# First norms that reuse the kept 1 / rms of the layer above, and a new order of NSA's fillers

## The chip, the cores and the metric

The kernel runs on one core of one Trainium2 chip. The metric is the device time of one execution in microseconds; the median of the timed runs is compared. Engines are named as in the profile: PE is TensorE's matmul, PEld its weight load, DVE VectorE, ACT ScalarE, POOL GpSimd, SP SyncE.

## The reference

A trunk of four layers over 256 tokens of width 1024, batch 1, in float32. Layers 0 and 3 mix tokens by differential attention ("diff"), layer 1 by native sparse attention ("NSA"), layer 2 by forgetting attention ("fox"). Each layer does the same around its mixer:

```python
for i in range(DEPTH):
    g = norm_g[i]
    h = rmsnorm(x, g[0])                    # the "first norm"
    y = mixer_i(h)                          # diff, NSA, fox, diff
    x = x + rmsnorm(y, g[1])
    y = sqrelu_mlp(rmsnorm(x, g[2]), mlp_w1[i], mlp_w2[i])
    x = x + rmsnorm(y, g[3])
    x = x + sigmoid(x @ ple_gate_w[i]) * (p[i] @ ple_w[i])   # the embedding

def rmsnorm(x, g):
    return x * lax.rsqrt(mean(x * x, axis=-1) + 1e-6) * g
```

Diff and fox project h to queries, keys and values (three blocks of 1024 columns; fox has 16 more for the forget gate, to which a bias is added before a log-sigmoid). NSA projects to 16 query heads, six blocks of 256 columns (keys and values for the compressed, selected and window branches) and 48 gates. Its compressed branch runs blocks of 32 tokens through a small two-layer network and takes a softmax over 15 of them; its three branches are added under the gates. With 256 tokens every selection block is chosen, so that the selected branch is plain causal attention.

Since every projection of h is linear and 1 / rms is one number per token, a projection can also be made of x times any per-token factor times g, if each token's result is corrected afterwards.

## The kernel before

Tokens lie in two tiles of 128 (t = 0, 1). Activations that go into a product are turned by TensorE transposes (L256) and split into a high and a low float32r part, `hT` (ACT L263 writes the high part, DVE L264 the low one). Weights arrive in `raw` tiles by SP's queue and are split in the same way by ACT (L150, `wh`) and DVE (L151, `wl`). A product is three passes (`three`, L173 to L175): high by high, low by high, high by low. PSUM is used in three rings of banks: `acc` (4), `pj` (2), `wk` (2).

The order of instructions on each engine follows from the order in which the program creates them and from the framework's scheduler, which moves an instruction ahead when it reckons it ready. `after(...)` puts each instruction of a block behind a given one on its own engine. Within a step the program's own lists set the order: `SEQ` for diff and fox (a letter for a projection, two digits for a softmax item, `p` for a step of the embedding's product `ple_proj`), `ORDN` for the items of NSA and `FILL` for what is done behind each NSA item:

- `s10`: first part of the compressed softmax of pair 1, token tile 0 (scores L959, bias L962, minimum, exp L968 on ACT, sum L970, gate, product L976 into a buffer `pc` that POOL clears, L974; there are two such buffers). `t10`: its transposes (L982), which free the buffer.
- `q1`: half of a query projection; `p`: a step of the embedding's product, for the later ones six matmuls and one ACT copy (L1145); `c`, `g`, `d`: the compressed branch's network; `O`: a weight unit of the output projection.

An NSA item computes scores (L1005), adds the bias and takes the minimum on DVE (L497), takes exp on ACT (L501); three steps later (`DP[1]` is 3) DVE scales by gate over sum (L1022), TensorE transposes (L1025), ACT copies out (L1027) and TensorE multiplies by the values (L1034).

The first norm of layer i + 1 is made in `prenorm` at the end of layer i, when the embedding's gate has been added to x (L1160): ACT squares and sums x (L220), POOL adds epsilon (L234) and takes the power of minus a half (L235), DVE multiplies x by g (L291), and the two halves are multiplied by 1 / rms on DVE (L295) or on ACT (L297), as the table `NORM` says for the layer. Then come the transposes. The result 1 / rms stays in `self.norm[t]`; the layer's second norm (`midnorm`, L309) already scales x by that kept number and corrects later.

Layer 0's first norm is special: its `hT` holds x times g without 1 / rms, and `self.cor[t]` holds 1 / rms. `cor_row` (L514 to L525) spreads both columns into a row `rb` along the tokens: the identity times `cor[t]` on DVE (L522), a matmul by ones (L523), a copy (L525). The copies out of PSUM then correct: V with `scale=cor[t]` on ACT (L534), queries and keys in `evac` by a DVE multiply by `rb` (L510). When `cor` is empty, as in layers 2 and 3, `evac` is an ACT copy (L512). NSA does not call `evac`: its queries (L947) and its selected and window keys (L990) are ACT copies.

Of the kernel before, what the change touches and what calls it, by code (L numbers as in the profile page):

```python
# [14 lines left out]
AF = mybir.ActivationFunctionType  # L15
ALU = mybir.AluOpType
AX = mybir.AxisListType

P = 128
D = 1024  # L20
S = 256
# [3 lines left out]
NH = 16  # L25
# [8 lines left out]
PACC = {0: 1, 1: 1, 2: 1, 3: 1}  # L34
PCB = 2
CW = 2
FILL = {-2: 'q0.c.p.q0.c', 1: 'p.g', 2: 'd0.q1.s01.d1', 3: 's00', 4: 't00.q1', 5: 's10.p.s11', 6: 'p', 7: 't01', 11: 't11.t10.O', 16: 'p'}
NORM = {0: 1, 1: 2, 2: 3, 3: 3}
MEP = 1
BANKS = dict(acc=('acc', 4), pj=('pj', 2), wk=('wk', 2))  # L40
MIXS = {0: {'v': 3, 'o': 2, 'd': 0, 'g': 0}, 1: {'v': 6, 'o': 2, 'd': 8, 'g': 1}, 2: {'v': 3, 'o': 6, 'd': 1, 'g': 0}, 3: {'v': 6, 'o': 2, 'd': 0, 'g': 0}}
# [45 lines left out]
class Trunk:  # L87
# [197 lines left out]
    def prenorm(self, t, g, hT, lag=()):  # L285

        nc = self.nc
        x = self.x[t]
        xn = self.s4([P, D])
        r = self.rms_kept(t, (self.rms(x), 0.0))  # L290
        nc.vector.tensor_tensor(xn, x, g, op=ALU.mult)  # L291
        for n in range(2):
            v = self.half(xn, n)
            if NORM[self.i] == 1 or NORM[self.i] == 3 and n:
                nc.vector.tensor_scalar(v, v, r, None, op0=ALU.mult)  # L295
            else:
                nc.scalar.activation(v, v, AF.Copy, scale=r)  # L297
        self.transpose_split(xn, hT[0], hT[1], t, lag=lag)

    def midnorm(self, t, g, hT, lag=()):  # L300

# [241 lines left out]
    def diff(self, i, ia, hT):  # L543
        nc, a = self.nc, self.a
        w_in = a["da_w_in"][ia]
        def between():
            if self.late is not None:
                self.late()
                self.late = None
            if self.row is None:  # L550
                self.bias_rows()

        vs = self.v_proj(w_in, 2 * D, hT, between)
        lam_init = 0.8 - 0.6 * math.exp(-0.3 * i)
# [112 lines left out]
    def fox(self, i, hT):  # L667
# [14 lines left out]
        lf = self.small([P, 2, NH])  # L682

        def forget():
            pf = self.pj()
            for k in range(KD):
                self.three(pf[:NH, :S], (wfh[:, k, :], wfl[:, k, :]), self.both(hT, k), k == 0, k == KD - 1)
            z = self.mid([NH, S])
            nc.vector.tensor_scalar(z, pf[:NH, :S], bf, None, op0=ALU.add)
            za = self.mid([NH, S])  # L690
            nc.vector.scalar_tensor_tensor(za, z, -1.0, z, op0=ALU.mult, op1=ALU.max)
            nc.scalar.activation(za, za, AF.Exp, scale=-1.0)
            nc.scalar.activation(za, za, AF.Ln, bias=1.0)
            nc.vector.scalar_tensor_tensor(za, z, 0.0, za, op0=ALU.min, op1=ALU.subtract)
            pl = self.wk()
            for t in range(2):
                nc.tensor.transpose(pl[:, t * NH : (t + 1) * NH], za[:, t * P : (t + 1) * P], self.ident[:NH, :NH])
            nc.vector.tensor_copy(lf.rearrange("p a b -> p (a b)"), pl[:, : 2 * NH])
# [145 lines left out]
    def nsa(self, i, hT):  # L844
# [21 lines left out]
        for t in range(2):  # L866
            y = self.acc()
            for k in range(KD):
                self.three(y[0][:, :256], self.tok(hT, k, t), w_vs[k], k == 0, k == KD - 1)
            for k in range(KD):  # L870
                self.three(y[1][:, :304], self.tok(hT, k, t), w_vw[k], k == 0, k == KD - 1)
            for z in range(2):
                nc.scalar.activation(vs[t][:, z], y[z][:, :256], AF.Copy)
            nc.vector.tensor_copy(gp[:, t, :], y[1][:, 256:304])
            o = self.pj()
            for k in range(KD):
                self.three(o, self.tok(hT, k, t), w_kv[k], k == 0, k == KD - 1)
            kv = self.m2([P, 512])
            nc.scalar.activation(kv, o, AF.Copy)
            pt = self.wk()  # L880
            for c in range(4):
                nc.tensor.transpose(pt[:, c * P : (c + 1) * P], kv[:, c * P : (c + 1) * P], self.ident)
            nc.scalar.activation(kvT[:, :, t * P : (t + 1) * P], pt.rearrange("p (c q) -> p c q", q=P), AF.Copy)
# [5 lines left out]
        def fill(n):  # L889
            for z in FILL.get(n, "").replace(".", " ").split():  # L890
                if z[0] == "c":
                    if "ph" not in cmp:
                        cmp["ph"] = self.cpsum()
                        cmp["up"] = self.compress_up(blks, cmp["ph"])
                    next(cmp["up"])
                elif z[0] == "g":
                    cmp["hid"] = self.compress_gelu(cmp["ph"])
                elif z[0] == "d":
                    self.compress_down(int(z[1]), cmp["hid"], (kcT, vcd)[int(z[1])])
                elif z[0] == "s":  # L900
                    soft2[z[1:]] = cmp_soft(int(z[1]), int(z[2]), qt[int(z[1])])
                    next(soft2[z[1:]])
                elif z[0] == "t":
                    next(soft2[z[1:]])
                    soft2[z[1:]] = None
                elif z[0] == "q":
                    next(qs[int(z[1])])
                elif z[0] == "p":
                    next(self.ple)
                elif z[0] == "Q":  # L910
                    q_load(int(z[1]))
                elif z[0] == "O":
                    self.early.append(self.unit(self.w_out, len(self.early), 1, 0, D))
            if n > 0:
                for ap, t in last:
                    if (ap, t) in po4 and soft2.get(f"{ap}{t}", 1) is None and n >= last[ap, t] + DP[i]:
                        finish(ap, t)

        qt, po4, soft2 = {}, {}, {}
        last = {(z[0], z[1]): n + 1 for n, z in enumerate(ORDN)}  # L920
        cmp = {}
        blks = [self.compress_blocks(kind, kvT[:, 2 * kind : 2 * kind + 2, :]) for kind in range(2)]
# [13 lines left out]
        def q_pair(ap):  # L936
            q_load(ap)
            us = q_ws[ap]
            q = qt[ap] = self.s4([P, 4, S])
            for r2 in range(2):  # L940
                o = self.pj()
                for rr in range(2):
                    r = 2 * r2 + rr
                    for k in range(KD):
                        st = [z[:, r, 2 * (k % 2) : 2 * (k % 2) + 2, :].rearrange("p g d -> p (g d)") for z in us[k // 2]]
                        self.three(o[:, rr * S : (rr + 1) * S], st, self.both(hT, k), k == 0, k == KD - 1)
                nc.scalar.activation(q[:, 2 * r2 : 2 * r2 + 2, :].rearrange("p a b -> p (a b)"), o, AF.Copy, scale=-0.125)  # L947
                yield

        qs = [q_pair(ap) for ap in range(2)]  # L950
# [36 lines left out]
        ksw = self.s4([P, 2, 2, S])  # L987
        for z, c in ((0, 512), (1, 1024)):
            o = self.lin_b(w_in, C0 + c, hT)
            nc.scalar.activation(ksw[:, :, z, :], o.rearrange("p (a b) -> p a b", a=2), AF.Copy)  # L990
            fill(z - 3)

        def item(ap, t, j, qt, nbs):
# [24 lines left out]
            for g2 in range(2):  # L1018
                e = es[:, g2]
                pt = self.wk()  # L1020
                for z in range(2):
                    nc.vector.tensor_scalar(e[:, z, :], e[:, z, :], rs[:, g2, z : z + 1], None, op0=ALU.mult)  # L1022
                    for kb in range(nk):
                        zz = (z * nk + kb) * P
                        nc.tensor.transpose(pt[:, zz : zz + P], e[:, z, kb * P : (kb + 1) * P], self.ident)  # L1025
                at = self.m2([P, 2, nk, P])
                nc.scalar.activation(at.rearrange("p a b c -> p (a b c)"), pt[:, : 2 * w], AF.Copy)  # L1027
                ats.append(at)
# [230 lines left out]
```

## Time and profile before

| what | value |
|---|---|
| median of 3 timed runs | 1384.98 us (1381.73 to 1389.02) |
| profiled execution | 1391.75 us, its span 1390.0 us |
| mean granted TensorE clock | 0.991 |
| busy: PE | 1370.6 us, 99% |
| busy: DVE | 906.8 us, 65% |
| busy: ACT | 756.9 us, 54% |
| busy: POOL | 52.9 us, 4% |
| read from HBM | 243.81 MB |

The span runs from the first to the last instruction. The profiled execution is one run of its own; the timed runs carry no profile. An engine counts as busy while an instruction of its is under way; matmuls overlap in the array, so that a busy PE may still be fed below its peak rate.

### The profile page before, as it was taken

How to read it: one execution, taken by the hardware profiler on the slowest of the kernel's cores; microseconds unless marked ns; L12 is line 12 of the kernel's file. 1: busy time of each engine (PE TensorE's matmuls, PEld its weight loads, DVE VectorE, ACT ScalarE, POOL GpSimd, SP SyncE). 2: the span in 40 equal slices, each digit the busy share in tenths (PEclk: the TensorE clock that was granted, in tenths of full speed). 3: DMA queues.
4: the chain of work that ended last, by engine and by line, in shares of the span. 5: the costliest groups of instructions: out<-in, count | busy, mean ns of one | idle time of the engine just before them, and what ended most of it. 6: DMA issues, size and time to landing. Idle time of an engine off the chain costs nothing.

```text
span 1390.0 us, 20343 instructions
## 1 busy us (share of the span) xinstructions
PE 1370.6 (99%) x7604; PEld 1138.5 (82%) x7604; DVE 906.8 (65%) x1636; ACT 756.9 (54%) x1268; POOL 52.9 (4%) x101
## 2 busy tenths in 40 slices
PE   8999999999999999999999999999999999999998
PEld 6987888888875678888878978888888987888887
DVE  6677765667556657656584576766576677766655
ACT  5556554456445755554465575645456566554443
POOL 1011000001000000000010000000001011000000
PEclk9999999999998999999999999999999999999999
DMA  8845765646772036655366644656554753665642
GB/s 267 263 144 154 237 198 188 190 141 195 193 258 95 23 119 223 199 186 183 121 214 197 225 133 154 214 183 198 190 187 124 232 169 102 219 210 170 204 141 76
DMA packets 144526, 247.28 MB, mean 178 GB/s; under 512 B 10195, under 2 KB 101243, under 8 KB 144428
## 3 DMA queue, kind: packets, MB, share of 16 engines
q1 hardware_dynamic: 134848, 235.26, 52.7%
q10 hardware_dynamic: 9580, 10.73, 2.5%
q8 instruction: 60, 0.98, 0.3%
q14 instruction: 38, 0.31, 0.1%
HBM read 243.81 MB, written 1.10 MB: 176 GB/s over the span
## 4 chain that ended last, share of the span: by engine, by line
PE 88%; issue 5%; DVE 2%; ACT 2%; POOL 2%; DMA 1%; SPq 0%; DVEq 0%; POOLq 0%; ACTq 0%
PE pj L182 13%; PE acc L173 13%; PE acc L174 13%; PE acc L175 13%; PE pj L183 7%; PE pj L173 7%; PE pj L175 6%; PE pj L174 6%; PE wk L256 2%; PE acc L627 1%; PE pj L1034 1%; PE acc L1005 1%; PE wk L1025 1%; DMA raw<-in_da_w_in_dram 1%; DVE wl L151 1%
## 5 line engine op out<-in xcount | busy, mean ns | idle before, releaser
L151 DVE TENSOR_TENSOR wl<-raw,wh 128x1024 fp32r<-128x1024 f32 x421 | 510.4, 1221 | 226.7 <-ACT wh L150 215.1
L150 ACT ACTIVATE wh<-raw 128x1024 fp32r<-128x1024 f32 x421 | 443.2, 1058 | 225.5 <-PE acc L174 106.4
L182 PE MATMUL pj<-big,wh 128*128 128x512 f32 x768 | 274.3, 401 | 0.0
L183 PE MATMUL pj<-big,wl 128*128 128x256 f32 x768 | 215.5, 281 | 0.0
L173 PE MATMUL acc<-wh,s 128*128 128x512 f32 x512 | 200.3, 392 | 0.0
L175 PE MATMUL acc<-wl,s 128*128 128x512 f32 x512 | 199.4, 390 | 0.0
L174 PE MATMUL acc<-wh,s 128*128 128x512 f32 x512 | 199.3, 390 | 0.0
L182 PEld LDWEIGHTS pj<-big,wh 128*128 128x128 f32 x768 | 144.2, 188 | 38.2 <-DVE m L1079 3.5
L183 PEld LDWEIGHTS pj<-big,wl 128*128 128x128 f32 x768 | 145.0, 189 | 0.9
L173 PE MATMUL pj<-big,wh 128*128 128x256 f32 x480 | 138.2, 288 | 0.5 <-ACT wh L150 0.5
L174 PE MATMUL pj<-big,wl 128*128 128x256 f32 x480 | 137.0, 285 | 0.5 <-DVE wl L151 0.5
L175 PE MATMUL pj<-big,wh 128*128 128x256 f32 x480 | 137.1, 286 | 0.0
L173 PE MATMUL acc<-wh,big 128*128 128x512 f32 (+2 forms) x344 | 131.6, 383 | 2.3 <-ACT wh L150 2.3
L174 PE MATMUL acc<-wh,big 128*128 128x512 f32 (+2 forms) x344 | 130.7, 380 | 0.0
L175 PE MATMUL acc<-wl,big 128*128 128x512 f32 (+2 forms) x344 | 129.7, 380 | 0.4 <-DVE wl L151 0.4
L175 PEld LDWEIGHTS acc<-wl,s 128*128 128x128 f32 x512 | 96.1, 188 | 20.4
L173 PEld LDWEIGHTS acc<-wh,s 128*128 128x128 f32 x512 | 96.0, 188 | 20.3 <-ACT s L1083 0.3
L174 PEld LDWEIGHTS acc<-wh,s 128*128 128x128 f32 x512 | 96.2, 188 | 19.3 <-DVE s L1084 0.2
L173 PEld LDWEIGHTS pj<-big,wh 128*128 128x128 f32 x480 | 92.4, 193 | 3.1 <-issue 1.2
L174 PEld LDWEIGHTS pj<-big,wl 128*128 128x128 f32 x480 | 92.4, 192 | 2.0 <-DVE wl L151 1.1
L175 PEld LDWEIGHTS pj<-big,wh 128*128 128x128 f32 x480 | 92.4, 192 | 0.4 <-issue 0.2
L501 ACT ACTIVATE s<-s,small 128x128 f32<-128x128 f32 (+1 forms) x160 | 70.8, 446 | 34.2 <-DVE small L497 25.4
(238 smaller groups left out, 1748.1 us busy)
## 6 DMA issues: line engine op xcount, KB each, us to landing
raw<-in_mlp_w_dram SPq DMA_DIRECT2D x256, 512.0 KB, 4.6
raw<-in_da_w_in_dram SPq DMA_DIRECT2D x48, 512.0 KB, 5.3
raw<-in_ple_gate_w_dram SPq DMA_DIRECT2D x32, 512.0 KB, 4.2
raw<-in_fox_w_in_dram SPq DMA_DIRECT2D x24, 512.0 KB, 4.6
raw<-in_nsa_w_in_dram SPq DMA_DIRECT2D x18, 512.0 KB, 4.5
raw<-in_da_w_out_dram SPq DMA_DIRECT2D x16, 512.0 KB, 4.2
g<-in_norm_g_dram SPq DMA_DIRECT2D x15, 512.0 KB, 6.1
nb<-row ACTq DMA_DIRECT2D x12, 512.0 KB, 6.7
```

Source lines behind the costliest of these rows:

```text
L150: self.nc.scalar.activation(wh, w, AF.Copy),
L151: self.nc.vector.tensor_tensor(wl, w, wh.bitcast(F32), op=ALU.subtract),
L173: mm(out, l[0], r[0], start=first, stop=False)
L174: mm(out, l[1], r[0], start=False, stop=False)
L175: self.mms.append(mm(out, l[0], r[1], start=False, stop=last))
L182: mm(out.rearrange("p (z n) -> p z n", z=2), l[0], aT[2][:, :, k, :], start=first, stop=False)
L183: mm(out[:, :S], l[1], a, start=False, stop=last)
L256: z = nc.tensor.transpose(pt[:, c * P : (c + 1) * P], src[:, (b + c) * P : (b + c + 1) * P], self.ident)
L501: nc.scalar.activation(e[:, b, :], e[:, b, :], AF.Exp, bias=m[:, b : b + 1], scale=-1.0, accum_out=s[:, b : b + 1])
L627: self.nc.tensor.matmul(sc[c][:, hh * w : (hh + 1) * w], q[cs, hh, qs], k[cs, hh, :w], start=True, stop=True)
L1005: nc.tensor.matmul(sc[g2][:, : 2 * w].rearrange("p (z k) -> p z k", z=2), qt[hs, r, qs], ksw[hs, ap, :, :w], start=True, stop=True)
L1025: nc.tensor.transpose(pt[:, zz : zz + P], e[:, z, kb * P : (kb + 1) * P], self.ident)
```

## The change

The first norms of layers 1 to 3 scale x by g and by the 1 / rms kept from the layer above (`p`), by one DVE scalar_tensor_tensor for each half, and are transposed at once. The layer's own 1 / rms (`r`) is taken afterwards by the same instructions as before, and `cor[t]` becomes r / p. Layers 1 to 3 then correct as layer 0 does: V and NSA's values by the scale of their ACT copies, NSA's gates by a DVE multiply, queries and keys by `evac` with the row `rb`, and the forget gate by one more DVE multiply. `cor_row` is called once more in each of these layers. `NORM` is gone.

In NSA, `FILL` changes: `s10` moves from step 5 to 6, `s11` from step 5 to 7, behind `t01`; the two embedding steps at 5 and 6 become `P` at 5 and 7, whose matmuls are put behind the last transpose of the last item that has been turned.

```diff
--- before.py
+++ after.py
@@ -34,8 +34,7 @@
 PACC = {0: 1, 1: 1, 2: 1, 3: 1}
 PCB = 2
 CW = 2
-FILL = {-2: 'q0.c.p.q0.c', 1: 'p.g', 2: 'd0.q1.s01.d1', 3: 's00', 4: 't00.q1', 5: 's10.p.s11', 6: 'p', 7: 't01', 11: 't11.t10.O', 16: 'p'}
-NORM = {0: 1, 1: 2, 2: 3, 3: 3}
+FILL = {-2: 'q0.c.p.q0.c', 1: 'p.g', 2: 'd0.q1.s01.d1', 3: 's00', 4: 't00.q1', 5: 'P', 6: 's10', 7: 'P.t01.s11', 11: 't11.t10.O', 16: 'p'}
 MEP = 1
 BANKS = dict(acc=('acc', 4), pj=('pj', 2), wk=('wk', 2))
 MIXS = {0: {'v': 3, 'o': 2, 'd': 0, 'g': 0}, 1: {'v': 6, 'o': 2, 'd': 8, 'g': 1}, 2: {'v': 3, 'o': 6, 'd': 1, 'g': 0}, 3: {'v': 6, 'o': 2, 'd': 0, 'g': 0}}
@@ -286,16 +285,15 @@
 
         nc = self.nc
         x = self.x[t]
+        p = self.norm[t][1]
         xn = self.s4([P, D])
+        for n in range(2):
+            nc.vector.scalar_tensor_tensor(self.half(xn, n), self.half(x, n), p, self.half(g, n), op0=ALU.mult, op1=ALU.mult)
+        self.transpose_split(xn, hT[0], hT[1], t, lag=lag)
         r = self.rms_kept(t, (self.rms(x), 0.0))
-        nc.vector.tensor_tensor(xn, x, g, op=ALU.mult)
-        for n in range(2):
-            v = self.half(xn, n)
-            if NORM[self.i] == 1 or NORM[self.i] == 3 and n:
-                nc.vector.tensor_scalar(v, v, r, None, op0=ALU.mult)
-            else:
-                nc.scalar.activation(v, v, AF.Copy, scale=r)
-        self.transpose_split(xn, hT[0], hT[1], t, lag=lag)
+        c = self.cor[t] = self.t([P, 1], "cor", 4)
+        nc.vector.reciprocal(c, p)
+        nc.vector.tensor_tensor(c, c, r, op=ALU.mult)
 
     def midnorm(self, t, g, hT, lag=()):
 
@@ -549,6 +547,8 @@
                 self.late = None
             if self.row is None:
                 self.bias_rows()
+            if i:
+                self.cor_row()
 
         vs = self.v_proj(w_in, 2 * D, hT, between)
         lam_init = 0.8 - 0.6 * math.exp(-0.3 * i)
@@ -682,11 +682,13 @@
         lf = self.small([P, 2, NH])
 
         def forget():
+            self.cor_row()
             pf = self.pj()
             for k in range(KD):
                 self.three(pf[:NH, :S], (wfh[:, k, :], wfl[:, k, :]), self.both(hT, k), k == 0, k == KD - 1)
             z = self.mid([NH, S])
-            nc.vector.tensor_scalar(z, pf[:NH, :S], bf, None, op0=ALU.add)
+            nc.vector.tensor_tensor(z, pf[:NH, :S], self.rb[:NH, :], op=ALU.mult)
+            nc.vector.tensor_scalar(z, z, bf, None, op0=ALU.add)
             za = self.mid([NH, S])
             nc.vector.scalar_tensor_tensor(za, z, -1.0, z, op0=ALU.mult, op1=ALU.max)
             nc.scalar.activation(za, za, AF.Exp, scale=-1.0)
@@ -870,13 +872,15 @@
             for k in range(KD):
                 self.three(y[1][:, :304], self.tok(hT, k, t), w_vw[k], k == 0, k == KD - 1)
             for z in range(2):
-                nc.scalar.activation(vs[t][:, z], y[z][:, :256], AF.Copy)
-            nc.vector.tensor_copy(gp[:, t, :], y[1][:, 256:304])
+                nc.scalar.activation(vs[t][:, z], y[z][:, :256], AF.Copy, scale=self.cor[t])
+            nc.vector.tensor_scalar(gp[:, t, :], y[1][:, 256:304], self.cor[t], None, op0=ALU.mult)
             o = self.pj()
             for k in range(KD):
                 self.three(o, self.tok(hT, k, t), w_kv[k], k == 0, k == KD - 1)
             kv = self.m2([P, 512])
-            nc.scalar.activation(kv, o, AF.Copy)
+            nc.scalar.activation(kv, o, AF.Copy, scale=self.cor[t])
+            if t == 1:
+                self.cor_row()
             pt = self.wk()
             for c in range(4):
                 nc.tensor.transpose(pt[:, c * P : (c + 1) * P], kv[:, c * P : (c + 1) * P], self.ident)
@@ -907,6 +911,9 @@
                     next(qs[int(z[1])])
                 elif z[0] == "p":
                     next(self.ple)
+                elif z[0] == "P":
+                    with self.after(turned[-1]):
+                        next(self.ple)
                 elif z[0] == "Q":
                     q_load(int(z[1]))
                 elif z[0] == "O":
@@ -916,7 +923,7 @@
                     if (ap, t) in po4 and soft2.get(f"{ap}{t}", 1) is None and n >= last[ap, t] + DP[i]:
                         finish(ap, t)
 
-        qt, po4, soft2 = {}, {}, {}
+        qt, po4, soft2, turned = {}, {}, {}, []
         last = {(z[0], z[1]): n + 1 for n, z in enumerate(ORDN)}
         cmp = {}
         blks = [self.compress_blocks(kind, kvT[:, 2 * kind : 2 * kind + 2, :]) for kind in range(2)]
@@ -944,7 +951,7 @@
                     for k in range(KD):
                         st = [z[:, r, 2 * (k % 2) : 2 * (k % 2) + 2, :].rearrange("p g d -> p (g d)") for z in us[k // 2]]
                         self.three(o[:, rr * S : (rr + 1) * S], st, self.both(hT, k), k == 0, k == KD - 1)
-                nc.scalar.activation(q[:, 2 * r2 : 2 * r2 + 2, :].rearrange("p a b -> p (a b)"), o, AF.Copy, scale=-0.125)
+                self.evac(q[:, 2 * r2 : 2 * r2 + 2, :], o, -0.125)
                 yield
 
         qs = [q_pair(ap) for ap in range(2)]
@@ -987,7 +994,7 @@
         ksw = self.s4([P, 2, 2, S])
         for z, c in ((0, 512), (1, 1024)):
             o = self.lin_b(w_in, C0 + c, hT)
-            nc.scalar.activation(ksw[:, :, z, :], o.rearrange("p (a b) -> p a b", a=2), AF.Copy)
+            self.evac(ksw[:, :, z, :], o)
             fill(z - 3)
 
         def item(ap, t, j, qt, nbs):
@@ -1022,7 +1029,7 @@
                     nc.vector.tensor_scalar(e[:, z, :], e[:, z, :], rs[:, g2, z : z + 1], None, op0=ALU.mult)
                     for kb in range(nk):
                         zz = (z * nk + kb) * P
-                        nc.tensor.transpose(pt[:, zz : zz + P], e[:, z, kb * P : (kb + 1) * P], self.ident)
+                        turned.append(nc.tensor.transpose(pt[:, zz : zz + P], e[:, z, kb * P : (kb + 1) * P], self.ident))
                 at = self.m2([P, 2, nk, P])
                 nc.scalar.activation(at.rearrange("p a b c -> p (a b c)"), pt[:, : 2 * w], AF.Copy)
                 ats.append(at)
```

## Rows read from the trace of the kernel before

**Rows 1.** The page: busy time by engine; granted clock in 40 slices.
```profile
PE 1370.6 (99%) x7604; PEld 1138.5 (82%) x7604; DVE 906.8 (65%) x1636; ACT 756.9 (54%) x1268; POOL 52.9 (4%) x101
...
PEclk9999999999998999999999999999999999999999
```

**Rows 2.** Waits of TensorE, whole span: total us, times, longest.
```profile
PE wk L256 <- ACT s L297: 2.7, 3, 2.1
...
PE wk L1025 <- DVE s L1022: 1.8, 2, 1.4
...
PE wk L256 <- DVE s L295: 1.0, 1, 1.0
```

**Rows 3.** Timeline, layer 1 to 2: start us, us, engine, [idle before].
```profile
713.07 1.22 DVE L291 TENSOR_TENSOR s<-x,g 128x1024 f32<-128x1024 f32 x1
...
714.17 3.61 POOL L234 TENSOR_SCALAR me<-small 128x1 f32<-128x1 f32 x1 [14.35 <-ACT m L220]
714.20 3.49 DVE L151 TENSOR_TENSOR wl<-raw,wh 128x1024 fp32r<-128x1024 f32 x3
...
718.46 1.33 ACT L297 ACTIVATE s<-s,r 128x512 f32<-128x512 f32 x2 [2.48 <-POOL r L235]
...
719.23 1.97 PE L256 MATMUL wk<-ident,s 128*128 128x128 f32 x8 [2.08 <-ACT s L297]
```

**Rows 4.** Windows: length, PE, PEld, DVE, ACT, POOL busy, clock, DMA.
```profile
411.92:439.23 27.31, 25.17 (x173) 19.73 (x173) 20.50 (x87) 15.59 (x43) 0.68 (x2) 1.00 0.51 176
...
439.23:452.88 13.65, 13.57 (x50) 6.85 (x49) 7.41 (x44) 7.26 (x26) 0.31 (x1) 0.50 0.13 39
719.12:722.54 3.42, 3.31 (x12) 3.02 (x13) 1.77 (x3) 3.40 (x6) 0.00 (x0) 0.50 0.69 241
752.00:776.00 24.00, 24.00 (x204) 23.66 (x201) 12.69 (x14) 10.78 (x14) 0.00 (x0) 1.00 0.89 293
```

**Rows 5.** Single lines: ns min/median/max (L523 by group: us, mean ns).
```profile
L309 DVE SCALAR_TENSOR_TENSOR s<-x,r,g x16: 742/745/750, 131.9 to 1184.6; 128x512 f32<-128x512 f32 x16
...
L523 PE MATMUL wk<-mid,mid 128*128 128x128 f32 x4 | 0.9, 300 | 0.1
...
L689 DVE TENSOR_SCALAR mid<-pj,small x1: 472/472/472, 740.3 to 740.3; 16x256 f32<-16x256 f32 x1
...
L534 ACT ACTIVATE s<-acc,r x4: 680/688/691, 24.2 to 36.8; 128x512 f32<-128x512 f32 x4
...
L510 DVE SCALAR_TENSOR_TENSOR s<-pj,rb x8: 681/684/692, 43.6 to 99.8; 128x512 f32<-128x512 f32 x8
...
  PEld acc L627: 0.2, 1
...
L512 ACT ACTIVATE s<-pj x16: 575/597/600, 760.2 to 1146.8; 128x512 f32<-128x512 f32 x16
```

**Rows 6.** Timeline of NSA's softmax stage, 432 to 452 us.
```profile
435.18 0.60 ACT L1145 ACTIVATE pp<-acc 128x512 f32<-128x512 f32 x1 [2.30 <-PE acc L175]
...
436.00 0.28 DVE L970 TENSOR_REDUCE small<-mid 128x8 f32<-128x120 f32 x1 [1.54 <-ACT mid L968]
...
438.36 1.30 PE L1025 MATMUL wk<-ident,s 128*128 128x128 f32 x8 [1.40 <-DVE s L1022]
...
449.87 0.35 DVE L976 TENSOR_TENSOR pc<-mid,small 128x60 f32<-128x60 f32 x2 [1.56 <-POOL pc L974]
```

**Rows 7.** Timeline of ACT and DVE, NSA, 374 to 388 us.
```profile
377.64 0.60 ACT L990 ACTIVATE s<-pj 128x512 f32<-128x512 f32 x1 [8.31 <-DMA s<-s]
...
379.51 0.58 DVE L779 TENSOR_TENSOR s<-s,small 128x240 f32<-128x240 f32 x1 [9.32 <-DMA s<-s]
...
379.55 0.60 ACT L990 ACTIVATE s<-pj 128x512 f32<-128x512 f32 x1 [1.32 <-PE pj L175]
...
380.42 3.47 DVE L779 TENSOR_TENSOR s<-s,small 128x240 f32<-128x240 f32 x7 [0.32 <-DMA s<-s]
```

**Rows 8.** Timeline of POOL, the first layer's first norm.
```profile
12.00 0.48 POOL L234 TENSOR_SCALAR me<-small 128x1 f32<-128x1 f32 x1 [9.86 <-ACT m L220]
```

## The prediction

> **What bounds the kernel now.** I read the page first: TensorE is busy for 99% of the span, and its granted clock is nine tenths or more in all but one of the forty slices [rows 1]. A change can therefore win only what TensorE loses (waits, or work at the lower clock) and costs whatever it adds to TensorE's own stream. The profiled execution took 1391.75 us, 6.8 us above the median of the timed runs (1384.98) and above all of them.
>
> I then listed TensorE's waits [rows 2]. The first norm's transposes (L256) wait 2.7 us for the scaled copy on ACT (L297) and 1.0 us for the one on DVE (L295): 3.7 us in all. NSA's transposes (L1025) wait 1.8 us for DVE, 1.4 us of it in one place.
>
> Third, the timeline between layers 1 and 2 shows what the norm waits for [rows 3]. x times g starts on DVE at 713.07, so x is there by then. The scaling on ACT starts only at 718.46, because POOL's add of epsilon to one number per partition took 3.61 us. It ended at 717.78, when a run of three weight splits on DVE ended (717.69). TensorE had by then stood still 2.08 us.
>
> Last, the windows show what a wait costs afterwards [rows 4]: 3.42 us at a granted clock of 0.50 behind that wait (1.2 instead of 2.4 GHz), and 13.65 us at 0.50 behind NSA's 1.4 us wait. These two stretches are the larger prize.
>
> **Norms: what is removed.** The new chain is x, then a scalar_tensor_tensor on each half, then the transposes; square, POOL and power leave it. Each half has the form of L309, 0.745 us [rows 5]. In the stretch shown DVE would start them at 713.07, where the multiply by g stood [rows 3], and end at 714.56, 2.6 us before TensorE began to wait (719.23 less 2.08 is 717.15). So I count all 3.7 us as removed. If another split of 1.22 us came between, 1.4 us of cover would remain. DVE does 1.49 us in place of 1.22 plus any scaling, and ACT loses six copies. The reciprocal and the multiply of the correction come behind these, on one column per partition, and delay only the correction row; that is the fourth rival's case.
>
> **The correction row: what is added.** Each of layers 1 to 3 gets one: two multiplies of the identity on DVE, two matmuls (four passes on TensorE, 0.9 us together [rows 5]), one copy. 3 times 0.9 is +2.7 us. The low bound is 0, if each fell into a wait; the high bound stands under the late-correction rival. V's and the NSA values' copies take a column as scale, which layer 0's copies show at 688 ns on ACT against 597 for a copy without one [rows 5]; the 0.09 us more of each is hidden while TensorE fills another bank, and would be 1.3 us over the 14 copies without that cover. Fox's forget gate gets one more small multiply, of L689's kind, 0.47 us [rows 5]. Its cover is the run of query and key products right behind, where TensorE is busy 24.00 of 24.00 us [rows 4]; without it the 0.47 us would be paid once.
>
> **Copies that change engine.** 22 copies out of PSUM (16 of fox and layer 3, 6 of NSA) go from ACT at 597 to DVE at 684 ns. Layer 0 already does this: its eight copies on DVE kept TensorE's loads waiting 0.2 us in all, and so did the sixteen on ACT [rows 5]. From below the cost is 0, from above 22 times 0.684, 15.0 us, if each held TensorE for its whole length. I take the near row: 0.2 times 22/8, +0.6 us.
>
> **NSA's order.** Before, both softmaxes of the second pair (s10, s11) come at step 5. The timeline shows the queue this makes [rows 6]: ACT's copy of the embedding product waits 2.30 us for TensorE, the exp of a compressed softmax stands behind it, DVE's sum idles 1.54 us for that exp, the scaling L1022 comes behind it on DVE, and TensorE's transposes wait 1.40 us for the scaling. After it, s10 stands at step 6, s11 at step 7 behind t01, and the products behind the transposes of their step. The same instructions are issued (12 product matmuls, two copies of about 0.6 us, the softmaxes' small operations, POOL's clearing of their buffer) and no DMA is moved. Putting t01 ahead of s11 also takes away the 1.56 us that DVE waited for POOL to clear a buffer t01 still held [rows 6]. What is late next is s11's own exp behind the second product's copy. I count the 1.4 us as removed.
>
> **The clock.** The 3.42 us at half speed did 1.7 us of work: 1.7 us is at stake. In the 13.65 us, DVE was busy 7.41 and ACT 7.26, and TensorE's 13.57 would be 6.8 at full clock [rows 4]; the floor is DVE's 7.4, a gain of 6.2. In the stretch before, at full clock, DVE was busy 20.50 of 27.31, three quarters; at that share the work takes 9.9 us, a gain of 3.8. From below the gain is 0. The full stake is 1.7 plus 3.8, 5.5 us. I take half, 2.75, because every timed run was quicker than the profiled one, by 2.7 to 10.0 us, so part of these stretches may not be in the median to be won.
>
> Sum: -3.7 - 1.4 - 2.75 + 2.7 + 0.6 = **-4.55 us**: 1387.2 against the profiled execution, **1380.4** against the median, 0.33% less. About 0.5% (6.9 us) is what a measurement of this kernel can tell from no change.
>
> **Rivals.** First, the clock is won back whole: -3.7 - 1.4 - 5.5 + 2.7 + 0.6 = -7.3 us, 1377.7. For it: the first pair's softmaxes stand one to a step, in a stretch at clock 1.00 (411.92 to 439.23) [rows 4]. Against it: that stretch had a query projection to fill TensorE, and the new one has only six product matmuls a step.
>
> Second, ending slower: NSA's selected and window keys are now copied by DVE, whose queue holds the eight adds of the compressed blocks ahead of them. Those wait for eight DMAs, until 379.51, and end at 383.89; ACT's first copy stood done at 378.24, and TensorE finished the second product near 379.5 [rows 7]. The next product needs the first one's bank. If the copy is queued behind all eight adds, the bank is free at 383.89 plus 0.68, 384.57: a new wait of 5.0 us (3.1 behind four adds), and 1.7 us at the lower clock as after the 2.08 us wait. That gives -4.55 + 6.7 = +2.15 us, 1387.1. Against it: if the copy goes ahead of the adds, DVE is idle for 9.32 us there and it costs nothing. It decides from 4.55 us of wait and clock together.
>
> Third, slower by more: DVE becomes the bound in the softmax stages. With the copies at 15.0 in place of 0.6, -4.55 + 14.4 = +9.85 us, 1394.8. The gain is gone from 5.15/22, 0.23 us per copy. Against it stands layer 0.
>
> Fourth, the wait moves from the transposes to the correction row, whose factor still comes through POOL. At the worst add seen, 3.61 instead of the 0.48 of the first one [rows 3, 8], 3.1 us late in one layer: -1.45 us, 1383.5. Against it: the row is due only after the first half's V product. The Trainium skill, GPSIMD Engine Reference, section Key points, says that GpSimd shares its SBUF interfaces with VectorE and contends with instructions that have two SBUF inputs. By that rule POOL's add lasts as long as such a run on DVE; the trace agrees, as the add ended 0.09 us behind the three splits.
>
> **Chances.** Forecast 0.36; clock whole 0.22; keys' copy blocked 0.22; DVE bound 0.12; correction late 0.08. The likeliest gives the time, 1380.4. Low end: both clock terms at their bound and the added work hidden, -3.7 - 1.4 - 1.7 - 6.2 = -13.0, 1372. High end: past the blocked copy and part way to DVE bound, 1391. Outside lie most of the DVE case and tails of the rest. Faster by over 0.5%: most of the whole-clock case and a quarter of the forecast's spread, 0.30. Slower by over 0.5%: the DVE case and a tail of the blocked copy, 0.16. Within: 0.54.
>
> **What would show it.** Right: no wait of L256 for L295 or L297; no low clock near 719; one cluster of compressed-softmax work per step, a shorter low clock after 439; about 0.9 us of L523's kind per layer. Wrong: a TensorE wait near 379 with the keys' copy on DVE behind the adds; TensorE waiting for evac's copies in fox or layer 3; TensorE waiting for the multiplies of the identity; or a low clock that moves to another step of NSA.

## The result, and the profile after

The changed kernel took **1395.15 us** (median of 10 runs, 1392.48 to 1405.87) against 1384.55 us before: ratio 1.0087, 95% interval 1.007 to 1.0104. It is 10.6 us slower. The forecast was 1380.4 us, 4.55 us less than the 1384.98 it started from, with a range that ended at 1391: the direction was wrong, and the time lies outside the range.

The page of the changed kernel (profiled execution 1398.98 us) hardly differs from that of before [rows 1]:

```profile
span 1397.2 us, 20397 instructions
...
PE 1376.1 (98%) x7616; PEld 1142.8 (82%) x7616; DVE 921.2 (66%) x1680; ACT 743.1 (53%) x1240; POOL 45.0 (3%) x104
...
PEclk9999999999999899999999999999999999999999
```

TensorE's waits, which answer to [rows 2] (in the changed kernel L255 is the transpose, L1029 the scaling, L1032 the transposes of a NSA item):

```profile
PE wk L1032 <- DVE s L1029: 4.6, 4, 2.4
...
PE wk L255 <- DVE mid L615: 1.6, 2, 0.9
PE acc L1012 <- DVE small L495: 1.5, 4, 0.9
```

The 3.7 us of waits for the first norms are gone, as forecast; what is left of L255 belongs to diff's output. But NSA's transposes now wait 4.6 us instead of 1.8, and its scores 1.5 us for DVE. Windows of NSA's softmax stage (columns as in [rows 4]):

```profile
411.92:440.63 28.71, 24.39 (x170) 18.43 (x169) 22.22 (x94) 16.33 (x48) 0.31 (x1) 1.00 0.48 167
440.63:447.46 6.83, 6.76 (x25) 4.48 (x24) 1.89 (x11) 3.53 (x12) 0.06 (x1) 0.50 0.00 0
447.46:461.11 13.65, 11.42 (x77) 6.21 (x77) 8.37 (x46) 7.69 (x26) 0.40 (x2) 1.00 0.23 78
461.11:474.76 13.65, 13.65 (x58) 7.91 (x57) 8.11 (x41) 7.20 (x25) 0.00 (x0) 0.50 0.01 2
```

There are two stretches at a granted clock of 0.50, of 6.83 and 13.65 us, where the profile of before had one of 13.65 us. The first follows this, in the timeline (s10's scores L966 and exp L975, scaling L1029, transposes L1032, the embedding's product L172):

```profile
436.80 1.10 PE L966 MATMUL wk<-s,s 128*128 128x64 f32 x8
...
437.94 0.35 DVE L969 TENSOR_TENSOR mid<-wk,s 128x60 f32<-128x60 f32 x2 [2.18 <-PE wk L966]
...
438.95 0.30 ACT L975 ACTIVATE mid<-mid 128x120 f32<-128x120 f32 x1 [1.89 <-DVE mid L974]
...
439.92 0.28 DVE L1029 TENSOR_SCALAR s<-s,small 128x128 f32<-128x128 f32 x1
...
440.35 1.32 PE L1032 MATMUL wk<-ident,s 128*128 128x128 f32 x4 [2.45 <-DVE s L1029]
...
441.31 0.78 PE L172 MATMUL acc<-wh,m 128*128 128x512 f32 x1
```

s10 stands alone at step 6. DVE does its chain first and comes to the next item's scaling at 439.92; TensorE has nothing else in its queue, since the product that ran in this place before is now held behind those very transposes. It waits 2.45 us, where it waited 1.40 in [rows 6]. The granted clock falls at 440.63. The second stretch follows this, in the timeline (L974 is s11's chain on DVE, ACTq L484 the load of the second pair's bias, L495 the minimum that reads it, L1012 the scores):

```profile
449.02 0.28 DVE L974 TENSOR_TENSOR mid<-mid,small 128x120 f32<-128x120 f32 x1
...
452.57 0.43 DVE L495 CUSTOM_DVE_ANT_0 s<-acc,nb 128x256 f32<-128x256 f32 x1
...
453.05 0.38 ACTq L484 DMA_DIRECT2D nb<-row  x1
...
453.46 1.67 ACTq L484 DMA_DIRECT2D nb<-row  x1
...
457.23 0.42 DVE L495 CUSTOM_DVE_ANT_0 s<-acc,nb 128x256 f32<-128x256 f32 x1 [3.04 <-DMA nb<-row]
...
459.70 0.42 DVE L495 CUSTOM_DVE_ANT_0 s<-acc,nb 128x256 f32<-128x256 f32 x1 [0.87 <-DMA nb<-row]
...
460.54 1.54 PE L1012 MATMUL acc<-s,s 64*128 64x512 f32 x2 [0.89 <-DVE small L495]
```

s11 at step 7 stands on DVE ahead of the first pair's last item. That item's minima free the bias buffers, so the second pair's two loads are issued only at 453.05 and 453.46, and DVE waits 3.04 and 0.87 us for their landing. TensorE's scores wait behind, and the granted clock falls at 461.11 for another 13.65 us. What of the loss hangs on each of these two waits, a profile alone does not say; the experiments part them.

### The profile page after: what moved, and what is told of

It is laid out like the page before. It is cut to its first block, busy times and chain, and to the rows that moved or that the text cites. A ratio compares the mean times of both kernels' runs of the same rounds, so it can differ in the third digit from the quotient of the medians.

```text
span 1397.2 us, 20397 instructions
## 1 busy us (share of the span) xinstructions
PE 1376.1 (98%) x7616; PEld 1142.8 (82%) x7616; DVE 921.2 (66%) x1680; ACT 743.1 (53%) x1240; POOL 45.0 (3%) x104
## 4 chain that ended last, share of the span: by engine, by line
PE 90%; issue 3%; ACT 2%; DVE 2%; DMA 1%; POOL 1%; ACTq 0%; DVEq 0%; POOLq 0%
PE acc L174 13%; PE acc L172 13%; PE acc L173 13%; PE pj L181 13%; PE pj L174 7%; PE pj L173 7%; PE pj L172 7%; PE pj L182 7%; PE wk L255 2%; PE acc L627 2%; PE pj L1041 1%; PE wk L1032 1%; PE acc L1012 1%; ACT wh L149 1%; PE wk L749 1%
## 5 line engine op out<-in xcount | busy, mean ns | idle before, releaser
L172 PE MATMUL acc<-wh,s 128*128 128x512 f32 x512 | 200.2, 391 | 0.0
L172 PE MATMUL pj<-big,wh 128*128 128x256 f32 x480 | 137.9, 287 | 0.5 <-ACT wh L149 0.5
L172 PE MATMUL acc<-wh,big 128*128 128x512 f32 (+2 forms) x344 | 131.5, 382 | 2.0 <-ACT wh L149 2.0
L172 PEld LDWEIGHTS acc<-wh,s 128*128 128x128 f32 x512 | 96.0, 188 | 20.3 <-ACT s L1090 0.3
L172 PEld LDWEIGHTS pj<-big,wh 128*128 128x128 f32 x480 | 92.3, 192 | 2.4 <-ACT wh L149 1.0
```

The lines of the kernel that those rows point to most:

```text
L172: mm(out, l[0], r[0], start=first, stop=False)
```

## The experiments

Each was timed against the kernel before on the same chip. Beside the ratio I use what each timed run also records, the mean granted clock: one minus it, times the span, is what full clock would have saved a TensorE that is always at work ("clock loss"). It is an upper estimate, and since the clock is recorded to 0.001, it comes in steps of 1.4 us. Differences in us are those of the medians, each to the runs of before on its own chip. The ratio with its 95% interval is taken over the runs and is not the quotient of the medians; the two can differ by over 1 us.

**The parts one by one.** The new norms with the old order of NSA:

```diff
-FILL = {... 5: 'P', 6: 's10', 7: 'P.t01.s11', ...}
+FILL = {... 5: 's10.p.s11', 6: 'p', 7: 't01', ...}
```

> The changed kernel with the filler list of before: new norms, correction rows and DVE copies stay; s10 and s11 stand at step 5 again and the embedding's products are not held behind transposes. Theory (the loss of 12 us is made by the new filler order in NSA's softmaxes, while the norms win what the sum said without the clock in NSA: -3.7 -1.7 +2.7 +0.6): 1380 to 1384 us, ratio to before 0.996 to 1.000. Rival (the DVE copies and correction rows are the loss): 1392 to 1397 us, ratio 1.006 to 1.009.

Measured: 1385.91 us against 1383.55, ratio 1.0015 (1.0004 to 1.0027). That is 2.4 us above the kernel before, where the changed one stands at 10.6. The norms don't carry the loss, but they win nothing either: the time lies above the theory's 1380 to 1384.

The new order alone, on the kernel before (its `FILL`, the list `turned` and `P`, nothing of the norms):

> The kernel before with the new filler list and the products held behind the transposes alone; norms, copies and filler bodies as before. Theory (the filler order is the loss): 1392 to 1398 us, ratio 1.006 to 1.010. Rival (the order is harmless or better by itself and the loss comes from the DVE copies and correction rows): at most 1385 us, ratio below 1.000.

Measured: 1392.66 us against 1383.55, ratio 1.0054 (1.0036 to 1.0071). The time lies in the theory's range, the ratio a little below its 1.006. The order alone is the larger part of the loss, which speaks for the theory.

**The two halves of the order.** The changed kernel with the products free, and the changed kernel with the softmaxes together again but the products held:

```diff
-5: 'P', 6: 's10', 7: 'P.t01.s11'
+5: 'p', 6: 's10', 7: 'p.t01.s11'      # e3_free
+5: 's10.P.s11', 6: 'P', 7: 't01'      # e4_together
```

> The changed kernel with the products of steps 5 and 7 no longer held behind the transposes; s10 at 6 and s11 at 7 stay. Theory A (TensorE runs out of work at step 6 because the products that filled it are held behind the transposes that wait): the 2.4 us wait there falls below 1 us, 1382 to 1388 us. Theory B (a single compressed softmax in a step of its own starves TensorE whatever the products do): the wait stays above 2 us, 1392 to 1398 us.

> The changed kernel with s10 and s11 at step 5 and the products at 5 and 6 as before, but still held behind the transposes. Theory A (holding the products is the cause): 1391 to 1398 us. Theory B (the one-by-one softmaxes are the cause): 1380 to 1386 us, as with the old list.

Measured: 1387.15 us, ratio 1.0033 (1.0015 to 1.0051), and 1387.75 us, ratio 1.0019 (1.0008 to 1.003). The first is as theory A said: the wait for the scaling falls to 0.4 us (in its place the scores wait 1.7 us, 1.5 of it at once, for the minima that stand behind s11). The second fits neither: with the products held TensorE waits 4.1 us for the scaling, 2.8 at the longest, and still the time stays below theory A's range. So neither theory stands alone: each half by itself, on top of the new norms' 1.0015, costs little or nothing, and both together cost 1.0087.

What only the two together make, in these profiles, is a late bias load. DVE's waits for it, between 420 and 500 us, in the changed kernel, in e2_fill and in e3_free (us in total, times, longest):

```profile
DVE s L495 <- DMA nb<-row: 3.9, 2, 3.0
...
DVE s L497 <- DMA nb<-row: 3.3, 2, 2.8
...
DVE s L495 <- DMA nb<-row: 0.9, 1, 0.9
```

In e4_together there is no such wait. In e3_free s11 stands in the same place as in the changed kernel, but its loads are issued at 446.14 and 448.54 us. Each of these is one profiled execution; the timed runs agree, as the two kernels with the late load stand 9.1 and 10.6 us above before and these two 3.6 and 4.2.

**The norms in two.** The new chain without its correction, and the correction without the new chain (old norms, a factor r times 1 / r in the same rows and copies):

```diff
-        r = self.rms_kept(t, (self.rms(x), 0.0))     # e5_chain: the changed prenorm
-        c = self.cor[t] = ...
+        self.rms_kept(t, (self.rms(x), 0.0))
```
```diff
         self.transpose_split(xn, hT[0], hT[1], t, lag=lag)   # e6_corr: the prenorm of before
+        c = self.cor[t] = self.t([P, 1], "cor", 4)
+        nc.vector.reciprocal(c, r)
+        nc.vector.tensor_tensor(c, c, r, op=ALU.mult)
```

> The kernel before with the new norm chain alone: first norms of layers 1 to 3 scale by the kept 1 / rms and are turned at once, and the correction is left out (no correction row, copies on ACT), so the projections of these layers are not corrected for the layer's own 1 / rms. Theory (the waits for POOL are worth what the profile showed): 3.7 us of waits go and half of the 1.7 us at the lower clock, 1378 to 1381 us, ratio 0.996 to 0.998. Rival (most executions wait less for POOL than the profiled one): 1381 to 1384 us, ratio 0.998 to 1.000.

> The kernel before with the correction alone: norms by the old chain, and on top the correction column (r times 1 / r, so 1), three correction rows, the 22 copies on DVE, the extra multiply in the forget gate; old filler list. Theory (the sum's +2.7 for the rows and +0.6 for the copies): 1386 to 1388 us, ratio 1.002 to 1.003. Rival (the DVE copies hold TensorE): 1390 to 1397 us, ratio above 1.005. Rival (the rows fall into waits): below 1385 us.

Measured: 1380.8 us against 1383.97, ratio 0.9973 (0.9962 to 0.9985), in the theory's range; and 1388.16 us, ratio 1.0034 (1.0022 to 1.0046), just above its theory's. The chain wins 3.2 us and its correction costs 4.2: together +1.0, and 2.4 was measured for both (e1_norms), within the intervals. The waits were worth what the profile said; the correction ate them.

With the copies back on ACT, so that rows, scales and the gate's multiply remain:

```diff
-        if self.cor:
+        if self.cor and self.i == 0:          # in evac
```

> The kernel with the correction alone (old norm chain, correction of 1), but the 22 copies back on ACT, so that the correction rows, V's scale and the gate's multiply are left as cost. If the rows are the cost (+2.7 by the sum): 1386 to 1388 us, as with the copies on DVE (1388.2). If the copies are: 1384 to 1385 us.

Measured: 1386.47 us against 1383.01, ratio 1.002 (1.0005 to 1.0034), which is 2.8 us by the ratio and 3.5 by the medians. The rows, scales and the gate's multiply are most of the correction's cost; what the copies add (1.0034 against 1.002) is within the two intervals. In the changed kernel's trace the rows' matmuls take TensorE 3.0 us, of which layer 0's four, there before, are 0.9 [rows 5]:

```profile
L521 PE MATMUL wk<-mid,mid 128*128 128x128 f32 x16 | 3.0, 286 | 0.1
```

So the twelve new ones take 2.1 us. The median clock loss of this run is also higher than that of before, 6.9 us against 4.1, and how much of the 2.8 is the rows' own work is not settled.

**The bias load.** The second pair reads the first pair's bias, so its loads and its own bias are left out; and, with nothing left out, s11 one step later, behind the item that frees the buffers:

```diff
-nbs[ap] = [self.bias_load(8 * ap + 4 * g2) for g2 in range(2)]
+nbs[ap] = nbs[0] if ap else [self.bias_load(8 * ap + 4 * g2) for g2 in range(2)]   # e7_onebias
-7: 'P.t01.s11'
+7: 'P.t01', 8: 's11'                                                                # e10_late_after
```

> The changed kernel with NSA's second pair reading the first pair's bias tiles, so that the second pair's bias is left out and its two loads are gone. Theory (the second half of the loss comes from the bias load, which now lands 3.9 us too late on DVE and sends TensorE to the lower clock near 461 us): 1386 to 1391 us. Rival (the late load costs nothing that the lower clock after step 6 would not cost anyway): 1393 to 1397 us.

> The changed kernel with s11 moved one step on, from 7 to 8, behind the last item of the first pair; nothing else. Theory (s11 ahead of that item delays the bias load): DVE's waits for the bias fall from 3.9 us to below 1 us and the time to 1386 to 1390 us, near the 1387.7 of the kernel without that load. Rival (the wait at step 6 with the products held is the whole cause, the load's lateness only follows from it): 1393 to 1397 us.

Measured: 1387.69 us against 1383.97, ratio 1.0033 (1.0021 to 1.0045), and 1387.38 us against 1383.01, ratio 1.003 (1.0019 to 1.0042). Without the loads 3.7 us of the loss are left; one step for s11 gives back 6.2 of the 10.6 us. The timeline of ACT's queue in e10_late_after shows the first load 2.8 us earlier than in the changed kernel, and the second 2.3 us behind it:

```profile
450.27 0.38 ACTq L484 DMA_DIRECT2D nb<-row  x1
...
452.53 0.37 ACTq L484 DMA_DIRECT2D nb<-row  x1
```

DVE no longer waits for them. The wait for the scaling is still 2.4 us at its longest, and the time is 2.0 us above that of the norms with the old order (4.4 against 2.4). The theories hold and their rivals fall: of the 8.2 us that the order adds to the norms, 6.2 go when the load comes in time, and 6.9 when it is left out. Most of that is clock, by the estimate above: the median clock loss is 11.1 us in the changed kernel, 6.2 and 6.9 in these two. It is not a share that adds up with others, since freeing the products (e3_free) gives back as much, and there too the load is nearly in time.

The same move on the kernel before:

```diff
-5: 's10.p.s11', 6: 'p', 7: 't01'
+5: 's10.p', 6: 'p', 7: 't01', 8: 's11'                                              # e9_late_before
```

> The kernel before with s11 alone moved, from step 5 to step 8, behind the last item that reads the first pair's bias (s10 stays at 5, t01 at 7, the products are free as before). If the place of s11 ahead of that item is what delays the bias load, its place behind it fills the load's time: 1379 to 1383 us, ratio 0.996 to 1.000. If any parting of s10 and s11 starves TensorE: 1386 to 1390 us, ratio 1.002 to 1.005.

Measured: 1387.58 us, ratio 1.0023 (1.0011 to 1.0035), as the second expectation said: the load was in time already (DVE waits for it in neither kernel), and parting the softmaxes costs. TensorE waits 1.2 us less for the scaling (0.6 instead of 1.8), but its scores now wait 1.8 us for the minima instead of 0.2. A version of it with the new norms in layers 2 and 3 alone:

```diff
     def prenorm(self, t, g, hT, lag=()):          # e12_best: e9_late_before and this
+        if self.i > 0:
+            return self.prenorm_kept(t, g, hT, lag)      # the changed kernel's prenorm
```

> The kernel before with s11 at step 8 and the new norms, rows and copies in layers 2 and 3 alone, NSA otherwise as before. From the runs so far: layers 2 and 3 win about 2.5 us by the chain and pay about 3 for the correction, so what is gained or lost comes from s11: 1379 to 1384 us. If it beats the kernel with s11 alone by over 1 us, the correction is cheaper in these layers than in NSA.

Measured: 1386.17 us, ratio 1.0025 (1.0011 to 1.004), above the expected range. By the medians it is 1.4 us below e9_late_before, by the ratio not, so that whether the correction is cheaper in these layers stays open.

**The profile of before, once more.**

> The kernel before, unchanged, profiled once more. If the profiled execution on which the forecast rests was an unusual one: a mean clock near 0.996, a span near 1382 us, POOL's add before the norms of layer 2 well under 3.6 us or no low clock near 719 us. If it was a usual one: 0.991 and 1390 us.

Measured: 1382.15 us, span 1380.4 us, mean clock 1.000. TensorE's waits, and the windows of the same stage:

```profile
PE wk L256 <- ACT s L297: 2.2, 3, 1.1
PE wk L1025 <- DVE s L1022: 1.8, 2, 1.4
...
PE wk L256 <- DVE s L295: 1.0, 1, 1.0
```

```profile
408.00:436.00 28.00, 25.81 (x177) 20.25 (x177) 21.99 (x90) 16.13 (x43) 0.66 (x2) 1.00 0.58 210
436.00:450.00 14.00, 13.57 (x99) 7.75 (x99) 10.42 (x61) 10.95 (x38) 0.31 (x1) 1.00 0.25 77
```

So the first profiled execution was the unusual one. The waits of [rows 2] are nearly all there, 1.40 us for NSA's scaling included, but no stretch at the lower clock follows. The 3.42 and 13.65 us of [rows 4] belonged to one execution: its clock loss was 12.5 us (0.009 of 1390), the median of 29 timed runs of before is 4.1. Only NSA's wait can be compared like for like. The one between layers 1 and 2 is itself shorter, 0.63 us instead of 2.08 [rows 3], because POOL's add beside the same three splits took 1.34 us instead of 3.61, and the add and the power behind it 2.8 instead of 4.2:

```profile
705.97 1.34 POOL L234 TENSOR_SCALAR me<-small 128x1 f32<-128x1 f32 x1 [14.35 <-ACT m L220]
706.01 3.49 DVE L151 TENSOR_TENSOR wl<-raw,wh 128x1024 fp32r<-128x1024 f32 x3
...
709.58 1.27 PE L256 MATMUL wk<-ident,s 128*128 128x128 f32 x8 [0.63 <-ACT s L297]
```

Here the bias loads were issued early and apart (ACT's queue):

```profile
442.65 0.38 ACTq L486 DMA_DIRECT2D nb<-row  x1
...
445.04 0.37 ACTq L486 DMA_DIRECT2D nb<-row  x1
```

**What was still open.** Two last runs: the add of epsilon on DVE in the kernel before, and the changed kernel with s11 at 8 and free products.

```diff
-        self.nc.gpsimd.tensor_scalar(me, ms[0], ms[1], EPS, op0=ALU.add, op1=ALU.add)
+        self.nc.vector.tensor_scalar(me, ms[0], ms[1], EPS, op0=ALU.add, op1=ALU.add)   # e13_add
-5: 'P', 6: 's10', 7: 'P.t01', 8: 's11'
+5: 'p', 6: 's10', 7: 'p.t01', 8: 's11'                                                # e14_late_free
```

> The kernel before with the add of epsilon in the first norms moved from POOL to DVE; the power stays on POOL, all else as before. If what the new chain won (3.2 us) is POOL's add being stretched beside DVE's splits (1.3 to 2.4 us each in the second profile of before, 0.4 to 0.5 without), most of it comes back without any correction: 1380 to 1382 us, ratio 0.997 to 0.999. If the whole chain of square, power and scaling is the wait, or DVE's own queue delays the add as long: 1382 to 1385 us.

> The changed kernel with s11 at step 8 and the products of steps 5 and 7 free of the transposes. If holding the products costs by itself once the bias load is in time: 1384 to 1386 us, 1.5 to 3 us below the 1387.4 of s11 at step 8 with held products. If not: 1387 to 1389 us.

Measured: 1386.04 us against 1384.95, ratio 1.001 (0.9999 to 1.0021): above both ranges, and nothing won. POOL's groups before (second profile: us, mean ns) and with the add on DVE:

```profile
L234 POOL TENSOR_SCALAR me<-small 128x1 f32<-128x1 f32 x8 | 11.2, 1397 | 86.6 <-ACT m L220 86.6
...
L235 POOL TENSOR_TENSOR r<-me,nhalf 128x1 f32<-128x1 f32 x8 | 6.2, 770 | 0.6
```

```profile
L235 POOL TENSOR_TENSOR r<-me,nhalf 128x1 f32<-128x1 f32 x8 | 12.4, 1546 | 93.2 <-DVE me L234 93.2
```

The add takes 0.146 us on DVE, but the power, now POOL's first operation there, is stretched from 0.77 to 1.55 us on average. Between layers 1 and 2 it lasts as long as the three splits beside it, and TensorE's waits for the scaled copies, 2.2 and 1.0 us in the second profile, come to 3.2 and 0.3:

```profile
706.26 3.48 DVE L151 TENSOR_TENSOR wl<-raw,wh 128x1024 fp32r<-128x1024 f32 x3
...
706.42 3.73 POOL L235 TENSOR_TENSOR r<-me,nhalf 128x1 f32<-128x1 f32 x1 [14.61 <-DVE me L234]
```

```profile
PE wk L256 <- ACT s L297: 3.2, 3, 1.8
...
PE wk L256 <- DVE s L295: 0.3, 1, 0.3
```

The last kernel took 1392.99 us, ratio 1.0065 (1.0035 to 1.0094), against both expectations. Its twelve runs reach from 1384.79 us at a mean clock of 1.0 to 1403.51 at 0.983, with one order of instructions. The windows of its profiled execution (1401.84 us, span 1400.0):

```profile
408.20:449.20 41.00, 38.24 (x254) 27.30 (x253) 30.46 (x132) 23.19 (x72) 1.05 (x3) 1.00 0.45 153
449.20:486.70 37.50, 37.44 (x168) 22.94 (x168) 17.08 (x86) 18.66 (x59) 0.00 (x0) 0.50 0.04 14
```

It spent 37.50 us on end at half clock, with TensorE busy nearly throughout. One kernel's runs lie 19 us apart, and their clock losses, 0 and 23.8 us, cover that and more. With each run's clock loss taken off, the median of this kernel is 1380.6 us and that of before 1380.4: as an estimate, its whole excess is clock. So freeing the products did not help here: the kernel stands 8.0 us above before, e10_late_after, with the products held, 4.4.

No version that leaves nothing out beat the kernel before.

## Why the prediction was wrong

**The norms' waits: right.** 3.7 us were counted as removed; they are gone from the trace, and the chain alone wins 3.2 us, as much as the waits come to in the second profile (2.2 and 1.0).

**The correction rows: right in size, in part by luck.** +2.7 us were counted; the new matmuls take 2.1 in the trace, and rows, scales and the gate's multiply measure +2.8 by the ratio, with an interval from 0.7 to 4.7 and some clock in it. **The copies on DVE:** +0.6 counted; 30 such copies, layer 0's eight among them, kept TensorE's loads waiting 0.4 us in the changed kernel's trace, and the timed difference is within the noise. So chain and correction together could never have won more than a fraction of a microsecond without the clock, as the terms -3.7, +2.7 and +0.6 say; measured is a loss of 2.4.

**NSA's order: this step failed.** "I count the 1.4 us as removed" supposed that a single softmax lets the scaling come sooner and that products behind the transposes cost nothing. In its place TensorE waits 4.6 us instead of 1.8, and DVE 3.9 us for the bias. The premise "no DMA is moved" was wrong in effect: the bias loads are issued later. I named s11's exp behind the second copy as what is late next; what was late was the scaling behind s10's own chain on DVE, with TensorE's only filler queued behind the waiting transposes, and the bias load, which the prediction does not name, behind s11. The prediction followed the buffer that POOL clears and missed the one that the first pair's minima free. Alone, the order costs 9.1 us (1.0054); on top of the norms it costs 8.2, of which one step for s11 gives back 6.2. What is left with the load in time, 2.0 us, is about what TensorE's longer wait for the scaling comes to there (4.1 us instead of 1.8).

**The clock: this step failed too.** The term of -2.75 us was taken from [rows 4] at half its size, because the timed runs were quicker. The second profile shows that the longer one is no fixed cost of the wait before it: the same 1.40 us wait, and no lower clock. In the median the clock loss rose from 4.1 us (the 29 runs timed beside the first experiments) to 11.1: 7.0 of the 10.6 us. These are not added to the order's 8.2 but lie mostly within them, since the norms with the old order have a median clock loss of 5.5. It was a cost to be feared, and I booked it as a gain.

**The rivals.** The clock won back whole: the reverse happened. The keys' copy behind the eight adds: half of it did happen, on DVE's timeline:

```profile
373.43 0.69 DVE L508 SCALAR_TENSOR_TENSOR s<-pj,rb 128x512 f32<-128x512 f32 x1 [3.88 <-PE pj L174]
379.38 0.58 DVE L781 TENSOR_TENSOR s<-s,small 128x240 f32<-128x240 f32 x1 [5.26 <-DMA s<-s]
380.32 3.49 DVE L781 TENSOR_TENSOR s<-s,small 128x240 f32<-128x240 f32 x7 [0.36 <-DMA s<-s]
383.73 0.68 DVE L508 SCALAR_TENSOR_TENSOR s<-pj,rb 128x512 f32<-128x512 f32 x1
```

The first copy (L508, 373.43) went ahead of the adds (L781), the second (383.73) stood behind all eight; TensorE shows no wait between 370 and 390, since its next product needed the first bank alone. DVE as the bound in the softmax stages: not by the copies, but DVE's order is what failed; that this rival's 1394.8 us lies beside the measured 1395.15 is luck. The late correction: TensorE's weight loads waited 0.5 us for the identity's multiplies in all, so no. Its remark that POOL's add lasts as long as the run of splits beside it held in the first profile and not in the second (1.34 us beside 3.49).

**Left open.** Why e14_late_free meets the long low clock and e10_late_after does not, though the loads are in time in both, was not settled, and so a late load is not the only way to that loss; nor how much of the two halves' cost in e3_free is the clock's (its runs fall in two groups, nine at 1384.80 to 1388.41 us and three at 1394.02 to 1396.79).

## What to carry to other kernels

A stretch at the lower clock in one profile is not a price that a wait has: compare the clock of several executions before it stands in a sum. When small work is moved between steps, follow every buffer that the work behind it frees, transfers above all, and not only the wait that the move is meant to take away. And work tied behind the very instruction that the queue waits for cannot fill that wait; by itself this cost little here, and together with a second delay it cost most of the loss.

## What the runs showed of the hardware

The same 1.40 us wait was followed by 13.65 us at 1.2 GHz in one execution of the kernel before and by none in another (1390.0 and 1380.4 us span). In the last kernel TensorE stayed at half clock for 37.50 us while it was busy for 37.44 of them.

POOL's operations on one number per partition are stretched beside DVE's splits, and by how much varies: beside the same run of three splits the add took 3.61 us in one execution and 1.34 in another, against 0.48 in the first norm [rows 8]. The Trainium skill, GPSIMD Engine Reference, section Key points, names contention of GpSimd with DVE instructions that have two SBUF inputs, as these splits have; the trace agrees. It is not bound to one operation: with the add taken away from POOL, the power took 1.55 us on average instead of 0.77.
